# A diffusion-backbone layer on one core: TensorE in program order, side work as generators between products, opening re-ordered

## The chip, the cores and the metric

The kernel runs on one core of one Trainium2 chip. The metric is device time in microseconds (us) of one execution, as the median of several runs. A profile is one further execution, recorded by the hardware; its time stands beside the median below. Engines are named as in the profile: PE is TensorE (PEld its weight loads), DVE is VectorE, ACT is ScalarE, POOL is GpSimd, SP is the engine that issues most DMAs.

## What is computed

One layer over 256 latent tokens and 256 context tokens of width 2048, in float32. Only the latent output is returned.

```python
mod_x = split((silu(c) @ w_mod + b_mod), 6)          # shift, scale, gate, twice
h  = modulate(x,   g_mix, mod_x[0], mod_x[1])        # RMSNorm * (1 + scale) + shift
hc = modulate(ctx, g_mix, mod_c[0], mod_c[1])
qa, ka, va, qb, kb, vb, rb, lrf, lrb, gate_a, gate_b = split(h @ w_in)   # the same for hc
qa, ka = rope(rms_norm(qa)), rope(rms_norm(ka))      # 16 query heads, 4 key heads, 128 wide
o_attn = windowed_attention(qa, ka, va, ctx_k, ctx_v, sink)              # |i-j| <= 128, plus all context keys
o_gla  = latent_gla(qb, kb, vb, gf, gb, states of the context)           # 4 heads, two directions
y = sigmoid(gate_a) * (o_attn @ w_attn_o) + sigmoid(gate_b) * ((rms_norm(o_gla) * silu(rb)) @ w_gla_o)
x = x + mod_x[2] * (y @ w_out)
x = x + mod_x[5] * conv_ffn(modulate(x, g_ffn, mod_x[3], mod_x[4]))      # 2 x 5632 wide, width-3 conv, SwiGLU
```

## The kernel before

**Products.** Every big projection is a float32 product made of three: `wsplit` loads a pair of weight blocks (2 x 128 rows by 512 columns, tile `raw`, seven buffers in the pool `wr`), and `split` (L61, L62) makes a rounded part `whi` on ACT and the rest `wlo` on DVE (three buffers each). The activations are split in the same way. `proj_nat` (L167) holds the tokens stationary and streams 512 weight columns; per pair of blocks it has 12 products for two 128-token rows, 24 for four (latent and context). `proj_T` (L186) holds the weights stationary and streams 256 or 2 x 256 tokens. Results collect in four accumulator banks (`acc`); side work has three banks of its own (`side`) and one (`main`).

**Stages.** The opening computes the first shift and scale on TensorE (`mod_both`: products `pm` over `mraw` tiles of `w_mod`, a DVE transpose, then a product `pcol`), transposes x and ctx (`ptx`), makes the norm factors (`token_rows`, product `pr`), and runs the projections QB, KB, VB over groups of block rows, `(0,2) (2,2) (4,4) (8,4) (12,4)`, adding each group's result to an SBUF tile (L394). The GLA stage runs four blocks (second half of KB, three of VB) with one GLA head beside each: `gla_A` builds decayed q and k over eight levels and multiplies them (`pa`, L534 for the levels and L599 for the context part), `gla_o` makes the outputs (`po`). Then KA and VA follow, with `norm_rope` on each bank of KA and a transpose `ptk` (L711). In the attention stage the blocks QA 1 to 3 and GA run with `attend` of one group of four heads beside each. RB and the merge follow: `rb_evac`, the four rounds of GA, `w_attn_o`, GB, `w_gla_o`, each result transposed by `to_T` (`pto`, L816), then `w_out`, the turn to the FFN (a `flush()` of all that is put off, norm, split) and the FFN.

**One instance of `attend`** (one group g, one block t of 128 queries): four times three score products `pS` (L751 to L753) and a masked copy with the row maximum on DVE (L755); small DVE steps (L759 to L761); on ACT the exponential of the sink (L762) and four exponentials with their sums (L764); sum and reciprocal (L766, L767) and four scalings by it (L769) on DVE; then, for four key blocks, four transposes `ptp` (L776), a split into `pth` and `ptl`, and three products `poa` (L782 to L784).

**What sets the order.** The program is written with `tick()` at the head of every pair of weight blocks. A tick counts down what `defer(n, ...)` has put off, takes steps of one generator `beside` (1.5 steps for each tick with GLA, 1.4 with attention), and issues steps of the background `bg_steps`. `mod_latent` is that background: the later shifts and gates as multiply-adds on DVE over `raw` tiles of `w_mod` (L266), out of the same pool as the weights. A generator that is not done at the end of its block is run out there. The order in which an engine then executes is chosen by a scheduler, for all engines, TensorE too; `high_priority` marks the weight splits. `chain` keeps the loads of the opening in program order on SP.

Of the kernel before, what the change touches and what calls it, by code (L numbers as in the profile page):

```python
# [8 lines left out]
F32 = mybir.dt.float32  # L9
# [21 lines left out]
def layer_kernel(ctx, tc, A, out):  # L31
# [6 lines left out]
    wr = pool(name="wr", bufs=7)  # L38
# [39 lines left out]
    x00 = M("x00", [P, D])  # L78
    nc.sync.dma_start(x00, A["x"][0][0:P, :])
# [22 lines left out]
    def columns(name, parts, eng=G):  # L102
        rows = sm.tile([P, P], F32, name="rows", tag="t128", bufs=2)
# [5 lines left out]
        pt = bank("pt_" + name, (P, P))  # L109
        PE.transpose(pt[:, :n], rows[:n, :], ident[:n, :n])  # L110
        t = cst.tile([P, n], F32, name=name)
        V.tensor_copy(t, pt[:, :n])
        return t

    c1 = columns("c1", [A["b_mod"][0], A["g_mix"][0], A["g_ffn"][0]], nc.scalar)
    bmod, gmix, gffn = c1[:, 0:96], c1[:, 96:112], c1[:, 112:128]

# [3 lines left out]

# [10 lines left out]

    def tick():

        for e in later:
            e[0] -= 1
        while later and later[0][0] < 0:
            later.pop(0)[1]()
        if beside:
            beside[2] += beside[1]  # L140
            while beside[2] >= 1.0:
                beside[2] -= 1.0
                next(beside[0], None)
        bg_rate[1] += bg_rate[0]
        while bg_rate[1] >= 1.0 and bg_steps:
            bg_rate[1] -= 1.0
            bg_steps.pop(0)()
# [17 lines left out]
    def proj_nat(w, r0, c0, kts, lhs, evac):  # L165

        banks = [acc.tile([P, 512], F32, name="acc", tag="acc") for _ in lhs]  # L167
        for k0 in kts[::2]:
# [3 lines left out]
            for i, l in enumerate(lhs):  # L172
                for k in range(nk):
                    kt = k0 + k
                    ahi, alo = l(kt)
                    PE.matmul(banks[i], ahi, hi[:, k, :], start=(kt == kts[0]), stop=False)  # L176
                    PE.matmul(banks[i], alo, hi[:, k, :], start=False, stop=False)  # L177
            for i, l in enumerate(lhs):
                for k in range(nk):
                    kt = k0 + k  # L180
                    PE.matmul(banks[i], l(kt)[0], lo[:, k, :], start=False, stop=(kt == kts[-1]))  # L181
# [3 lines left out]
    def proj_T(w, c0, kts, rhs, evac):  # L185
# [4 lines left out]
        for k0 in kts[::2]:  # L190
            tick()
            nk = min(2, kts[-1] + 1 - k0)
            hi, lo = wsplit(w[k0 * P:(k0 + nk) * P, c0:c0 + 512])
            for part in range(2):
                for f in range(4):
                    for k in range(nk):
                        kt = k0 + k
                        w_ = (lo if part else hi)[:, k, f * P:(f + 1) * P]
                        for i, r in enumerate(rhs):
# [3 lines left out]
                            PE.matmul(o, w_, ahi, start=(kt == kts[0] and b == 0 and part == 0),  # L203
                                      stop=(kt == kts[-1] and part == 1), skip_group_check=True)
                            if part == 0:
                                PE.matmul(o, w_, alo, start=False, stop=False, skip_group_check=True)  # L206
        for i in range(len(banks)):
            evac(i, banks[i])
# [4 lines left out]
    def mod_both(part, t0, n, dst):  # L213
# [5 lines left out]
        def step(k0):  # L219
# [8 lines left out]
            if k0 == KT - nk:  # L228
                tr = W2("fb", "mtr", [P, n, 4, 32])
                V.transpose(tr.rearrange("p a b c -> p (a b c)"), a[0])  # L230
                pc = bank(f"pcol{part}_{t0}", (32, n * 4, 2))
                PE.matmul(pc, sel[:, 0:32], tr.rearrange("p a b c -> p (a b) c")[:, :, 0:2], start=True, stop=True)
                pv = pc.rearrange("p (a b) c -> p b c a", b=4)
                for b4 in range(4):
                    V.tensor_copy(dst[32 * b4:32 * b4 + 32, :, t0:t0 + n], pv[:, b4, :, :])
                b0 = part * 16 + t0
                d = dst[:, :, t0:t0 + n]
                V.tensor_tensor(d, d, bmod[:, b0:b0 + n].unsqueeze(1).to_broadcast([P, 2, n]), op=ALU.add)

        return [lambda k0=k0: step(k0) for k0 in range(0, KT, nk)]  # L240

    def mod_latent(parts):
# [11 lines left out]
        def step(i):  # L254
# [13 lines left out]
            if k0 == KT - 2:  # L268
# [15 lines left out]
                defer(3, out)  # L284
# [48 lines left out]
    groups = [(0, 2), (2, 2), (4, 4), (8, 4), (12, 4)]  # L333
    mods = [mod_both(0, t0, n, shift1) + mod_both(1, t0, n, scale1) for t0, n in groups]
# [4 lines left out]

    def load_tokens(s):  # L340
        ss = sm.tile([P, 2], F32, name="ss0", tag="ss0", bufs=2)
        for t in range(2):
            x_ = x00
            if s or t:
                x_ = M(f"x{s}{t}", [P, D])
                load(x_, A["ctx" if s else "x"][0][t * P:(t + 1) * P, :])
            if t:
                V.scalar_tensor_tensor(junk, x_, 1.0, x_, op0=ALU.mult, op1=ALU.mult, accum_out=ss[:, t:t + 1])
            else:
                S.activation(junk, x_, AF.Square, accum_out=ss[:, t:t + 1])  # L350
            for g in range(4):
                pt = bank("ptx", (P, 4, P), side=True)
                for k in range(4):
                    kt = g * 4 + k
                    PE.transpose(pt[:, k, :], x_[:, kt * P:(kt + 1) * P], ident)
                dst = xr[2 * s + g // 2][:, (g % 2) * 4:(g % 2) * 4 + 4, t * P:(t + 1) * P]
                if g % 2:
                    V.tensor_copy(dst, pt)
                else:
                    S.activation(dst, pt, AF.Copy)  # L360
        rrow1.append(token_rows("fa", f"rrow{s}", rms_scale(ss, D, [P, 2])))
# [35 lines left out]
    hh, hl = [], []  # L397
    for gi, (t0, n) in enumerate(groups):
        kts = ALL[t0:t0 + n]
        if gi == 0:  # L400
            load_tokens(0)
            for f in mods[0]:
                f()
        while bg_steps:
            bg_steps.pop(0)()
        if gi + 1 < len(groups):
            bg_steps.extend(mods[gi + 1])
            ticks = 4 * ((n + 1) // 2)
            bg_rate[:] = [1.4 * len(bg_steps) / ticks + 0.01, 0.0]
        for s in range(2):  # L410
            if gi == 0:
                if s:
                    load_tokens(1)
                hh.append([M(f"h{s}{h}hi", [P, 8, T], F32R) for h in range(2)])
                hl.append([M(f"h{s}{h}lo", [P, 8, T], F32R) for h in range(2)])
            affine_group(s, t0, n)
            if s == 0:
                if gi == 0:
                    qb0 = [W2("fc", "qb0", [P, 512]) for _ in range(4)]
                for j in range(2):  # L420
                    proj_T(w_in, QB + j * 512, kts, [h_all(0)], add_to(lambda i, j=j: qb0[2 * j + i], gi == 0))
        if gi == 0:
            kbt = M("kb0", [P, 4, 512])
            vb0 = M("vb0", [P, 4, 512])
        proj_T(w_in, KB, kts, [h_all(0), h_all(1)], add_to(lambda i: kbt[:, i, :], gi == 0))
        proj_nat(w_in, 0, VB, kts, h_xc, add_to(lambda i: vb0[:, i, :], gi == 0))

    chain.clear()


    cw0 = columns("cw0", [A["conv_w"][0, 0], A["b_gate_f"][0], A["b_gate_b"][0]])
    cw1 = columns("cw1", [A["conv_w"][0, 1]])
    cw2 = columns("cw2", [A["conv_w"][0, 2]])
# [572 lines left out]
```

## Time and profile before

| | |
|---|---|
| median of 3 runs | 2054.3 us (2053.26 to 2057.96) |
| the profiled execution, own time | 2061.47 us |
| its span | 2059.7 us |
| PE busy | 1998.4 us, 97% |
| DVE busy | 1399.2 us, 68% |
| ACT busy | 932.7 us, 45% |
| HBM read, mean rate | 409.63 MB, 200 GB/s |
| DMA in the first 1/40 of the span | 346 GB/s |

Busy times are shares of the span. The stages lie at about 0 to 214 us (opening), 214 to 527 (GLA), 527 to 575 (KA and VA), 575 to 800 (attention), 800 to 1275 (RB and merge), 1275 to 1325 (turn to the FFN), 1325 to the end (FFN). Matmuls are pipelined: the time listed for one is longer than the distance to the next, and a TensorE that is listed busy may still run at a lower granted clock.

### The profile page before, as it was taken

Reading aid. Unit: us, or ns where it says so; the run is one execution under the profiler, and the core shown is the slowest. Engines: PE = TensorE matmul, PEld = TensorE weight load, DVE = VectorE, ACT = ScalarE, POOL = GpSimd, SP = SyncE. Lnnn points to the kernel's source line nnn. Section 1 sums busy time; section 2 is a strip of 40 time slices with the busy share of each in tenths; the row PEclk is TensorE's granted clock in tenths of the full one; section 3 lists DMA queues with packets and bytes.
Section 4 is the critical chain, followed back from the end, with each engine's and each line's share of the span. In section 5 each row is a group of like instructions: output and inputs, shape, how many; then the busy total and the mean of one; then the engine's idle time right before and its main releaser. Section 6 shows DMA issues by size and latency. Waiting matters only on the chain.

```text
span 2059.7 us, 30028 instructions
## 1 busy us (share of the span) xinstructions
PE 1998.4 (97%) x11792; PEld 1727.0 (84%) x11792; DVE 1399.2 (68%) x2149; ACT 932.7 (45%) x1306; POOL 38.9 (2%) x62
## 2 busy tenths in 40 slices
PE   6999999999999999999999999899999999999998
PEld 4778888888787777788788888899999889999987
DVE  4657577887758888777776455877787455556654
ACT  4323464552345665444344444544445334445532
POOL 0001000001000000000000000000000000000000
PEclk8999999999999999999999999899999999999999
DMA  9977322346553466788886766576776666666563
GB/s 346 360 261 217 95 82 83 92 134 203 162 153 113 135 194 198 254 274 273 275 267 218 230 211 205 177 252 226 235 260 208 201 192 191 182 182 183 184 214 112
DMA packets 214350, 413.71 MB, mean 201 GB/s; under 512 B 12548, under 2 KB 21092, under 8 KB 213184
## 3 DMA queue, kind: packets, MB, share of 16 engines
q1 hardware_dynamic: 212320, 406.89, 62.0%
q0 software_dynamic: 1360, 4.74, 0.8%
q8 instruction: 92, 1.51, 0.3%
q14 instruction: 50, 0.41, 0.1%
q10 hardware_dynamic: 528, 0.17, 0.0%
HBM read 409.63 MB, written 2.11 MB: 200 GB/s over the span
## 4 chain that ended last, share of the span: by engine, by line
PE 78%; DVE 9%; DMA 8%; ACT 2%; issue 2%; DVEq 0%; POOL 0%; ACTq 0%; SPq 0%
PE acc L203 20%; PE acc L176 13%; PE acc L177 13%; PE acc L181 13%; PE acc L206 10%; DMA raw<-in_w_mod 8%; DVE wlo L62 3%; DVE macc L266 3%; PE pm L227 1%; PE pa L534 1%; PE po L620 1%; ACT whi L61 1%; PE pa L599 1%; PE ptp L776 1%; PE poa L782 0%
## 5 line engine op out<-in xcount | busy, mean ns | idle before, releaser
L61 ACT ACTIVATE whi<-raw 128x1024 fp32r<-128x1024 f32 x568 | 601.0, 1060 | 833.9 <-PE acc L177 512.4
L62 DVE TENSOR_TENSOR wlo<-raw,whi 128x1024 fp32r<-128x1024 f32 x568 | 693.9, 1226 | 359.6 <-ACT whi L61 327.0
L203 PE MATMUL acc<-h2h,whi 128*128 128x256 f32 x1408 | 347.4, 284 | 1.5 <-ACT h2h L377 1.5
L206 PE MATMUL acc<-h2l,whi 128*128 128x256 f32 x1408 | 346.9, 284 | 0.0
L266 DVE SCALAR_TENSOR_TENSOR macc<-raw,ccol,macc 128x512 f32<-128x512 f32 x240 | 180.3, 751 | 137.3 <-DMA raw<-in_w_mod 133.9
L203 PEld LDWEIGHTS acc<-h2h,whi 128*128 128x128 f32 x1408 | 271.5, 193 | 2.0 <-ACT h2h L377 1.8
L206 PEld LDWEIGHTS acc<-h2l,whi 128*128 128x128 f32 x1408 | 271.4, 193 | 0.2
L203 PE MATMUL acc<-h2h,wlo 128*128 128x256 f32 x1408 | 198.5, 284 | 1.7 <-DVE wlo L62 1.7
L203 PEld LDWEIGHTS acc<-h2h,wlo 128*128 128x128 f32 x1408 | 182.4, 193 | 1.9 <-DVE wlo L62 1.9
L176 PE MATMUL acc<-whi,h00hi 128*128 128x512 f32 x352 | 141.0, 400 | 0.9 <-DVE kb L394 0.6
L176 PE MATMUL acc<-whi,h01hi 128*128 128x512 f32 x352 | 139.8, 397 | 0.0
L177 PE MATMUL acc<-whi,h00lo 128*128 128x512 f32 x352 | 139.7, 397 | 0.0
L177 PE MATMUL acc<-whi,h01lo 128*128 128x512 f32 x352 | 137.8, 391 | 0.0
L176 PE MATMUL acc<-whi,ah 128*128 128x512 f32 x352 | 137.1, 389 | 0.0
L177 PE MATMUL acc<-whi,al 128*128 128x512 f32 x352 | 137.0, 389 | 0.0
L181 PE MATMUL acc<-wlo,h00hi 128*128 128x512 f32 x352 | 98.2, 394 | 0.0
L181 PE MATMUL acc<-wlo,h01hi 128*128 128x512 f32 x352 | 96.9, 393 | 0.5 <-DVE wlo L62 0.5
L181 PE MATMUL acc<-wlo,ah 128*128 128x512 f32 x352 | 94.1, 389 | 0.0
L176 PEld LDWEIGHTS acc<-whi,h00hi 128*128 128x128 f32 x352 | 66.7, 190 | 14.7 <-ACT h00hi L377 0.7
L181 PEld LDWEIGHTS acc<-wlo,h00hi 128*128 128x128 f32 x352 | 66.1, 189 | 13.9 <-DVE wlo L62 0.3
L181 PEld LDWEIGHTS acc<-wlo,ah 128*128 128x128 f32 x352 | 66.1, 188 | 13.8
L176 PEld LDWEIGHTS acc<-whi,ah 128*128 128x128 f32 x352 | 66.1, 188 | 13.7
(369 smaller groups left out, 3267.7 us busy)
## 6 DMA issues: line engine op xcount, KB each, us to landing
raw<-in_w_in SPq DMA_DIRECT2D x208, 512.0 KB, 4.4
raw<-in_w_up SPq DMA_DIRECT2D x176, 512.0 KB, 3.9
raw<-in_w_mod SPq DMA_DIRECT2D x128, 512.0 KB, 4.2
raw<-in_w_down SPq DMA_DIRECT2D x88, 512.0 KB, 4.3
mraw<-in_w_mod SPq DMA_DIRECT2D x32, 1024.0 KB, 12.0
raw<-in_w_attn_o SPq DMA_DIRECT2D x32, 512.0 KB, 4.7
raw<-in_w_gla_o SPq DMA_DIRECT2D x32, 512.0 KB, 5.1
raw<-in_w_out SPq DMA_DIRECT2D x32, 512.0 KB, 4.1
```

The lines of the kernel that those rows point to most:

```text
L61: S.activation(hi, src, AF.Copy)
L62: V.tensor_tensor(lo, src, hi.bitcast(F32), op=ALU.subtract)
L176: PE.matmul(banks[i], ahi, hi[:, k, :], start=(kt == kts[0]), stop=False)
L177: PE.matmul(banks[i], alo, hi[:, k, :], start=False, stop=False)
L181: PE.matmul(banks[i], l(kt)[0], lo[:, k, :], start=False, stop=(kt == kts[-1]))
L203: PE.matmul(o, w_, ahi, start=(kt == kts[0] and b == 0 and part == 0), stop=(kt == kts[-1] and part == 1), skip_group_check=True)
L206: PE.matmul(o, w_, alo, start=False, stop=False, skip_group_check=True)
L227: PE.matmul(a[0][q:q + 32, :], cS[:, kt, :], raw[:, k, :], start=(kt < 4), stop=(kt >= 12))
L266: V.scalar_tensor_tensor(a[0], raw[:, k, :], ccol[:, kt:kt + 1], a[0], op0=ALU.mult, op1=ALU.add)
L534: PE.matmul(pa[:, t, :], k2[:, dt, t * P:(t + 1) * P], q2[:, dt, tq * P:(tq + 1) * P], start=(dt == 0), stop=(dt == 1))
L599: PE.matmul(pa[:, t, :], kk[:, dt, t * P:(t + 1) * P], qq[:, dt, :], start=(i == 0 and dt == 0), stop=(i == 1 and dt == 1))
L620: PE.matmul(po, x_, y_[:, s, :], start=(n == 0), stop=(n == 11))
```

## The change

`manual_schedule` takes TensorE out of the scheduler's hands: it executes in the order of the program. The other engines are still scheduled. `tick()` now also comes between products, after every 6 of 512 columns or 12 of 256, so a pair of blocks has 2 or 4 ticks. Generators state how many ticks they pause (`yield 4.5`), several can run at once, and they run on over the ends of blocks: one for all of GLA, one for all of attention. Four-row projections take their rows in two pairs, both parts of a pair before the next. The delays of `defer` grow with the number of ticks, and due entries run whatever their place in the list. In the opening the loads and products of the first modulation come ahead of x, the second 4-row group is two groups of 2, VB stands ahead of KB, `pcol` comes a step after its `pm` products (`end`), and the small transposes of `columns` are put off. The scaling of the probabilities and the first copy of `at` go from DVE to ACT. The pool `wr` has six buffers.

```diff
-    wr = pool(name="wr", bufs=7)
+    wr = pool(name="wr", bufs=6)
...
     def tick():
...
-        while later and later[0][0] < 0:
-            later.pop(0)[1]()
-        if beside:
-            beside[2] += beside[1]
-            while beside[2] >= 1.0:
-                beside[2] -= 1.0
-                next(beside[0], None)
+        due = [e for e in later if e[0] < 0]
+        later[:] = [e for e in later if e[0] >= 0]
+        for e in due:
+            e[1]()
+        for e in list(beside):
+            e[2] += e[1]
+            while e[2] > 0:
+                n = next(e[0], None)
+                if n is None:
+                    beside.remove(e)
+                    break
+                e[2] -= n
...
+            for i2 in range(0, len(lhs), 2):
+                for part in range(2):
+                    for i in range(i2, min(i2 + 2, len(lhs))):
...
+                            if mms % 6 == 0 and mms < len(lhs) * nk * 3:
+                                tick()
...
-    groups = [(0, 2), (2, 2), (4, 4), (8, 4), (12, 4)]
+    groups = [(0, 2), (2, 2), (4, 2), (6, 2), (8, 4), (12, 4)]
+
+    def both_parts(t0, n):
+        (s0, e0), (s1, e1) = (mod_both(part, t0, n, dst) for part, dst in ((0, shift1), (1, scale1)))
+        return s0 + s1[:1] + [e0] + s1[1:] + [e1]
...
-        V.tensor_scalar(at, pa, 2.0, None, op0=ALU.mult)
+        S.activation(at, pa, AF.Copy, scale=2.0)
...
             prev = q2, k2
-            yield
+            yield 2.75
...
         V.tensor_tensor(kg, kg, kc, op=ALU.mult)
-        yield
+        yield 4
...
-    bg_rate[:] = [0.3, 0.0]
+    bg_rate[:] = [0.08, 0.0]
...
-        defer(1 + i // 2, turn)
+        defer(8 + 4 * i, turn)
...
                 sc.append(s_)
+                yield 0.34
...
             for h in range(4):
-                V.tensor_scalar(sc[h], sc[h], ds_[:, h:h + 1], None, op0=ALU.mult)
-            yield
-            yield
+                S.activation(sc[h], sc[h], AF.Copy, scale=ds_[:, h:h + 1])
+            yield 4.5
...
-        beside[:] = [attend(g, qTs), 1.4, -2.9]
-        qTs = qa_block(g + 1) if g < 3 else ga_block()
-        for _ in beside[0]:
-            pass
-        beside.clear()
-
-
-    bg_rate[0] = 0.52
+    run(attend_all())
+    for g in (1, 2, 3):
+        qa_block(g)
+    proj_nat(w_in, 0, GA, ALL, h_x, lambda t, b: S.activation(m1[0][t], b, AF.Copy))
+
+
+    bg_rate[0] = 0.24
...
-            defer(1 + t, lambda: to_T(s_, gh, gl, j, t))
+            defer(4 + 2 * t, lambda: to_T(s_, gh, gl, j, t))
...
-    bg_rate[:] = [0.36, 0.0]
+    bg_rate[:] = [0.18, 0.0]
...
+            ctx.enter_context(tc.manual_schedule(engines={mybir.EngineType.PE}))
```

Three places show what moves. The first is attention's third instance (second group, first query block) on TensorE, around its first transposes `ptp`; `acc` is the projection, `wlo` and `whi` its weights. Before:

```order
L181 MATMUL acc<-wlo,h00hi 128x512 x4
L776 MATMUL ptp<-ident,s 128x128
L176 MATMUL acc<-whi,h00hi 128x512
L177 MATMUL acc<-whi,h00lo 128x512
L776 MATMUL ptp<-ident,s 128x128
L176 MATMUL acc<-whi,h00hi 128x512
L776 MATMUL ptp<-ident,s 128x128
L177 MATMUL acc<-whi,h00lo 128x512
L776 MATMUL ptp<-ident,s 128x128
```

And of the change, at the same place:

```order
L201 MATMUL acc<-wlo,h01hi 128x512 x4
L852 MATMUL ptp<-ident,s 128x128 x4
L197 MATMUL acc<-whi,h01hi 128x512
L198 MATMUL acc<-whi,h01lo 128x512
L197 MATMUL acc<-whi,h01hi 128x512
```

The four transposes of a key block stood between products and now follow one another. From the instance's last score product to its first transpose there were 37 products of the projection and there are 24 (30 in the last five of the eight instances).

On ACT, the same instance, from the exponential of the sink `es`; `s` are the scores, `y` and `sq` the norm of another bank. Before, and then of the change:

```order
L762 ACTIVATE es<-es 128x4
L764 ACTIVATE s,ds<-s,mx 128x512 x3
L61 ACTIVATE whi<-raw 128x1024
L764 ACTIVATE s,ds<-s,mx 128x512
L685 ACTIVATE y<-acc 128x512
L687 ACTIVATE sq<-y 128x512
L61 ACTIVATE whi<-raw 128x1024
```

```order
L837 ACTIVATE es<-es 128x4
L61 ACTIVATE whi<-raw 128x1024
L839 ACTIVATE s,ds<-s,mx 128x512 x3
L61 ACTIVATE whi<-raw 128x1024
L839 ACTIVATE s,ds<-s,mx 128x512
L844 ACTIVATE s<-s,ds 128x512 x4
L61 ACTIVATE pth<-ptp 128x512 x2
```

The four scalings (L844) are new on ACT, behind the last exponential, and two weight splits stand among the exponentials.

The third place is the start of the program on TensorE, up to the first product of the projections (`h00hi`). Before, and then of the change:

```order
L355 MATMUL ptx<-ident,x_147 128x128 x16
L327 MATMUL pr<-dg,ones 128x128 x2
L227 MATMUL pm_0_193<-mraw,cS 32x256 x16
L232 MATMUL pcol_0_216<-mtr,sel 32x16
L227 MATMUL pm_0_223<-mraw,cS 32x256 x16
L232 MATMUL pcol_0_246<-mtr,sel 32x16
L227 MATMUL pm_2_270<-mraw,cS 32x256 x8
L203 MATMUL acc<-h00hi,whi 128x256
```

```order
L257 MATMUL pm_0_118<-mraw,cS 32x256 x16
L257 MATMUL pm_0_141<-mraw,cS 32x256 x8
L112 MATMUL pt_c_152<-ident,rows 128x128
L265 MATMUL pcol_0_155<-mtr,sel 32x16
L257 MATMUL pm_0_141<-mraw,cS 32x256 x8
L395 MATMUL ptx<-ident,x_175 128x128 x16
L395 MATMUL ptx<-ident,x_176 128x128 x16
L265 MATMUL pcol_0_229<-mtr,sel 32x16
L360 MATMUL pr<-dg,ones 128x128 x2
L229 MATMUL acc<-h00hi,whi 128x256
```

The modulation's products moved ahead of the transposes of x, each `pcol` behind further work, and `pr` next to the first product of the projections.

More of the change, by code (lines that the diff above doesn't have):

```diff
@@ L131, in flush, with run, drain @@
             later.pop(0)[1]()
+    def run(gen, pace=1.0, wait=0.0):
+        beside.append([gen, pace, -wait])
+    def drain():
+        while beside:
+            for _ in beside.pop(0)[0]:
+                pass
     def tick():
@@ L404, in layer_kernel @@
         while bg_steps:
             bg_steps.pop(0)()
+        if gi == 0:
+            new_h(0)
+            qb0 = [W2("fc", "qb0", [P, 512]) for _ in range(4)]
         if gi + 1 < len(groups):
[L407 to L421, printed above, removed]
+            more = both_parts(*groups[gi + 1])
+            bg_rate[:] = [1.4 * len(more) / (6 * n), 0.0]
+            if gi:
+                bg_steps.extend(more)
@@ L603, in gla_A @@
         res.extend((ats, atc))
+        yield 2
     def gla_o(h, a, vh, vl):
@@ L743, in attend @@
         for t in range(2):
+            while (g, t) not in ready:
+                yield 1
+            qT = qTs[g]
             mx = sm.tile([P, 4], F32, name="mx", tag="mx")
```

309 lines of the change are left out of this document (181 added, 128 removed).

## The prediction

> **What bounds the kernel now.** I read the head of the profile page first, then the busy time by stage, then TensorE's waits by line. Its section 4 follows back from the last instruction what released each step.
>
> ```profile
> span 2059.7 us, 30028 instructions
> PE 1998.4 (97%) x11792; PEld 1727.0 (84%) x11792; DVE 1399.2 (68%) x2149; ACT 932.7 (45%) x1306; POOL 38.9 (2%) x62
> ...
> PE 78%; DVE 9%; DMA 8%; ACT 2%; issue 2%; DVEq 0%; POOL 0%; ACTq 0%; SPq 0%
> ```
>
> TensorE is busy 97% of the span. A change that leaves the matmuls alone can gain only what TensorE waits, and whatever makes it wait longer is added to the time. The next table cuts the span at the stages: opening (to 214 us), GLA (214 to 527), KA and VA (527 to 575), attention (575 to 800), RB and merge (800 to 1275), the turn to the FFN, the FFN.
>
> ```profile
> 0.00:28.00 28.00, 14.54 (x122) 10.32 (x122) 11.54 (x37) 9.40 (x15) 0.88 (x5) 0.93 0.99 316
> 28.00:75.00 47.00, 40.96 (x293) 32.15 (x294) 23.39 (x53) 19.49 (x34) 2.09 (x4) 0.86 0.98 355
> 75.00:214.00 139.00, 136.41 (x962) 111.82 (x961) 92.67 (x164) 43.26 (x58) 6.87 (x11) 1.00 0.79 266
> 214.00:527.00 313.00, 304.49 (x1759) 259.18 (x1757) 235.00 (x426) 154.50 (x303) 26.36 (x37) 1.00 0.40 118
> 527.00:575.00 48.00, 42.99 (x187) 34.30 (x186) 28.50 (x65) 15.46 (x28) 0.00 (x0) 0.93 0.43 131
> 575.00:800.00 225.00, 223.16 (x1030) 175.51 (x1028) 182.11 (x368) 127.72 (x221) 0.00 (x0) 1.00 0.53 156
> 800.00:1275.00 475.00, 466.50 (x2084) 380.84 (x2083) 321.01 (x384) 205.25 (x225) 1.65 (x3) 0.99 0.74 242
> 1275.00:1325.00 50.00, 41.90 (x254) 37.93 (x253) 38.15 (x68) 23.90 (x38) 0.00 (x0) 0.86 0.56 172
> 1325.00:2060.00 735.00, 727.44 (x5117) 685.00 (x5116) 466.82 (x589) 333.77 (x388) 1.06 (x2) 1.00 0.64 203
> ```
>
> After the stretch come its length, the busy time of PE, PEld, DVE, ACT and POOL, the granted clock, the DMA share and GB/s. The length less the PE column is what can be won: 13.5 us up to 28 us (there the loads run at 0.99 of the DMA engines), 6.0, 2.6, 8.5 in GLA, 5.0 in KA and VA, only **1.8 in attention**, 8.5 in RB and merge. The turn (8.1) and the FFN (7.6) keep their code but for the ring and the ticks. So attention has nothing to give, and its DVE is the busiest of any stage (182 of 225 us). TensorE's waits by line, with total, number and longest:
>
> ```profile
> PE pr L327 <- DVE dg L326: 9.3, 3, 3.7
> ...
> PE ptk L711 <- DVE sq L700: 5.0, 1, 5.0
> PE pa L599 <- DVE kf L592: 4.9, 4, 2.1
> PE pcol L232 <- DVE mtr L230: 4.8, 7, 0.9
> PE pto L816 <- DVE sr L826: 3.9, 1, 3.9
> PE pa L534 <- DVE q L554: 3.4, 4, 1.5
> PE pto L816 <- DVE m L857: 3.2, 2, 2.3
> ...
> PE ptp L776 <- DVE s L769: 0.7, 1, 0.7
> ```
>
> **The change, part by part.** The work hardly changes: 32 score scalings and the four `at` copies go from DVE to ACT, two-row groups add 12 accumulations on DVE, two table loads are added on ACT. What changes is where TensorE's side work stands between the products of a projection, so each part is a sum of covers. One instance of attention (one group and one 128-query block, eight in all) gives the prices. It runs from the last score product `pS` to the first transposed probabilities `ptp`:
>
> ```profile
> 666.25 0.40 PE L753 MATMUL pS<-kTh,qT 128*128 128x512 f32 x1
> ...
> 668.05 0.68 DVE L755 CUSTOM_DVE_ANT_0 s<-pS,att 128x512 f32<-128x512 f32 x1
> ...
> 669.76 0.19 ACT L762 ACTIVATE es<-es 128x4 f32<-128x4 f32 x1
> ...
> 670.56 0.71 ACT L764 ACTIVATE s<-s,mx 128x512 f32<-128x512 f32 x1
> ...
> 671.97 1.04 ACT L61 ACTIVATE whi<-raw 128x1024 fp32r<-128x1024 f32 x1
> ...
> 672.40 0.39 PE L177 MATMUL acc<-whi,h00lo 128*128 128x512 f32 x1
> ...
> 672.92 0.71 ACT L764 ACTIVATE s<-s,mx 128x512 f32<-128x512 f32 x1
> ...
> 673.76 0.39 PE L177 MATMUL acc<-whi,h00lo 128*128 128x512 f32 x1
> ...
> 674.38 0.18 DVE L767 RECIPROCAL ds<-ds 128x4 f32<-128x4 f32 x1
> ...
> 674.60 1.68 DVE L769 TENSOR_SCALAR s<-s,ds 128x512 f32<-128x512 f32 x4
> ...
> 675.14 0.33 PE L776 MATMUL ptp<-ident,s 128*128 128x128 f32 x1
> ...
> 676.87 0.58 ACT L61 ACTIVATE pth<-ptp 128x512 fp32r<-128x512 f32 x1
> ...
> 677.91 0.68 DVE L62 TENSOR_TENSOR ptl<-ptp,pth 128x512 fp32r<-128x512 f32 x1
> ```
>
> The two projection products quoted start 1.36 us apart with six starts from one to the other: a pitch of 0.227 us (the 0.39 is a pipelined latency). The softmax chain takes 674.60 - 666.25 = 8.35 us to the start of the scaling and 10.0 to its end at 676.28. Before, 37 products (8.4 us) stood in front of `ptp`, and further ones between its four transposes, so each later scaling was covered too.
>
> *Attention, the deciding term.* In the new order 24 products stand there in the first three instances and 30 in the other five, and the four transposes then follow without a product between them. The cover, with the score product itself, is 25 x 0.227 = 5.7 us, or 31 x 0.227 = 7.0 us. The scaling is now four ACT passes. The nearest row is the ACT copy of a 128x512 tile, 0.58, against 1.68 / 4 = 0.42 on DVE, so the last scaled tile is ready 8.35 + 4 x 0.58 = 10.7 us after the score product. TensorE stands still for 3 x (10.7 - 5.7) + 5 x (10.7 - 7.0) = 33.5 us; less the 0.7 and a few tenths that it waits today, **+32.5 us**. Behind the waiting transposes stand the whole projection, `poa` and the next scores, since TensorE runs in program order; nothing slips past. Low end: the two weight splits of ACT inside the chain (1.04 each) are out of the way because the ring of split weights is full, 8.6 us, which gives 3 x 2.9 + 5 x 1.6 = 16.7. High end: the chain is 1.5 us longer, as where the q norm of the next block stands between the reductions on DVE, 45.5. I take the middle, because it is the chain that was measured, with its splits.
>
> *Opening.* A first projection's `pcol` now has eight `pm` products of the second one ahead of it, and the first `pr` has a `pcol` and transposes. Half of the 4.8 us on `pcol` goes. Of the 6.0 + 2.6 us idle in 28 to 214 us another 2.8 may go by loads that stand nearer to their use, but the DMA engines are at 0.98 there and the bytes are the same. The x tiles now load behind four blocks of `w_mod`, so the `pr` chain (9.3 us in three, 3.1 each) and the copy of the last transposes (0.6) stand in the open ahead of the first main product; a fifth block of 1.05 MB (2.9 us at 355 GB/s) no longer loads ahead of it: +0.8. Together -2.4 - 2.8 + 0.8 = **-4.5 us** (rounded up). The 12 new accumulations (12 x 0.68 = 8.2 us of DVE) lie beside products while DVE has the room that 23.39 of 47 us shows. Ends: -9 (all of the idle time), +4 (those 8.2 us come through, less what is gained).
>
> *GLA.* A pause ahead of the `kf` products becomes 4 ticks of 6 products, 24 x 0.227 = 5.4 us, where one step was 24 x 0.227 / 1.5 = 3.6 us: 1.8 us more for each of four, which is nearly all of the 4.9 on L599. Of the 3.4 on L534 a little goes with `at` on ACT. **-5 us**, ends -8.3 (both rows) and +4 (DVE, at 235 of 313 us, falls behind the even pace of the levels).
>
> *KA and VA.* `ptk` is put off by 8 ticks or more (8 x 6 x 0.227 = 10.9 us), so its 5.0 us goes, and with it the slow products behind it (rows below, 2.2 us). The fourth bank's norm still has to wait for one of six `fc` buffers, for which I leave 2 us. **-5 us**, ends -7 and -1.
>
> *RB and merge.* `pto` of the two blocks is now released 4 and 6 ticks into the next projection (5.4 and 8.2 us) where it was 1 and 2 ticks of 12 products (2.7 and 5.4). That is up to 2.7 us more cover for the waits of 3.9 and 3.2, so 4.3 us go, and 1.7 of slow clock behind the first. **-6 us**, ends -9 and -1. The weight ring of six instead of seven costs nothing I can see: loads land some 4 us after issue and six pairs are 6 x 2.7 = 16 us of products.
>
> **Sum:** -4.5 - 5 - 5 - 6 + 32.5 = +12 us. The profiled execution took 2061.47 us, its span 2059.7 and 1.8 around it, 7.2 above the median of the runs, 2054.3. I add the difference to both: some 2073 in a profile like this one, **2066 us** as a median.
>
> [...] What follows a stall of TensorE is seen in the stage of KA (first four rows, after `ptk`) and of RB (after `pto`):
>
> ```profile
> 537.50:540.00 2.50, 0.00 (x0) 0.00 (x0) 2.50 (x15) 0.22 (x2) 0.00 (x0) 0.87 0.39 142
> 540.00:542.50 2.50, 0.65 (x3) 0.65 (x4) 2.50 (x6) 0.60 (x1) 0.00 (x0) 0.50 0.00 0
> 542.50:545.00 2.50, 2.50 (x9) 2.02 (x8) 2.38 (x4) 1.12 (x2) 0.00 (x0) 0.50 0.00 0
> 545.00:547.50 2.50, 2.50 (x10) 2.00 (x9) 1.27 (x2) 1.48 (x2) 0.00 (x0) 0.76 0.00 0
> ...
> 860.00:862.50 2.50, 2.50 (x10) 2.02 (x9) 2.50 (x4) 0.60 (x1) 0.00 (x0) 0.54 0.81 241
> 862.50:865.00 2.50, 2.50 (x13) 2.05 (x11) 1.26 (x4) 1.06 (x1) 0.00 (x0) 0.78 0.72 220
> ```
>
> The granted clock falls to 0.50 and 0.54 and stays low for some 5 us. The loss is the share not granted: 0.65 x 0.5 + 2.5 x 0.5 + 2.5 x 0.24 = 2.2 us behind the 5.0 us wait, 2.5 x 0.46 + 2.5 x 0.22 = 1.7 behind the 3.9 us wait. [...]
>
> **The rivals.**
> - *The chain is shorter than its cover needs (faster).* Three of the four reductions are now done before the last score product, and with the split ring full ACT goes straight through the exponentials. Without the two splits the chain is 8.6 us; the fourth reduction began 1.8 us after its score product, behind other DVE work; take off 1.4 of that, and it is 7.2: stalls of 3 x 1.5 + 5 x 0.2 = 5.5 us, 4.5 more than now. Then the 20.5 us gained elsewhere decide: 2054.3 + 4.5 - 20.5 = 2038. It decides from the chain at which eight stalls cost 21 us, 2.6 each over a mean cover of 6.5: below about **9.1 us** the change is faster. For it: the spread scores. Against it: 10.0 us measured with the cheaper DVE scaling.
> - *The clock falls at every attention stall (slower).* Stalls of 3.7 and 5.0 us lie about the 3.9 that brought the clock to 0.54. Eight times 1.8 us is 14 us: 2066 + 14 = 2080. Against it: the attention stall is broken by transposes as each scaling ends, and may not read as one idle stretch. [...]
> - *DVE becomes the bound in the opening and GLA.* The 8.2 us of accumulations come through and the 9.5 us gained in the two stages stay away: 2066 + 17.7 = 2084. Against it: DVE's 50% and 75%.
>
> That the order stays what it was is excluded by the rows of the order shown with the change.
>
> **How the numbers follow.** Forecast 0.46, with its own range 2054 to 2078; shorter chain 0.29; clock 0.19; DVE 0.06. The 80% range goes from 2037, just under the shorter chain's time, to 2092, where the high end of attention (45.5 for 33.5) and the clock meet. A measurement of this kernel tells 0.2% (4.1 us) from no change. Faster by more: 0.26, from the shorter chain. Within: 0.03 from it and 0.07 from the forecast's lower edge, 0.10. Slower: 0.39 + 0.19 + 0.06 = 0.64.
>
> **What would show it.** Right: a new leading row, `ptp` waiting for the ACT scaling some 30 us in eight times or more, attention's PE idle time above 25 us, and `ptk`, `pto` and `kf` gone from the waits. Wrong: `ptp` below 20 us in all (first rival), PEclk under 0.95 in attention (second), PE idle time grown in the opening or GLA (third).

## The result, and the profile after

The changed kernel took 2138.9 us (2131.94 to 2142.25, 4 runs) against 2056.0 for the kernel before (2053.26 to 2057.96, 4 runs): a ratio of 1.040, interval 1.037 to 1.043. It is **slower by 83 us**, outside the range of the prediction. The profiled execution of it was the quickest of its four, 2131.94 us with a span of 2130.2, and that of the kernel before, 2061.47 us, was slower than its four runs, so the two profiles differ by only 70.5 us of span.

The head of the page after the change:

```profile
span 2130.2 us, 30255 instructions
PE 2025.0 (95%) x11860; PEld 1742.2 (82%) x11860; DVE 1399.0 (66%) x2139; ACT 955.6 (45%) x1340; POOL 41.2 (2%) x62
...
PEclk9999999999999898999999999999999999999999
...
PE 73%; DMA 10%; DVE 10%; ACT 5%; issue 2%; DVEq 0%; ACTq 0%; POOL 0%; POOLq 0%
```

TensorE's busy time grew by 26.6 us for nearly the same work (68 small products more) and its idle time from 61.3 to 105.2 us. ACT, 2% of the chain before, has 5%. Now the stages, cut where the same part of the program stands in both (KA ends some 3 us later, VA 8, everything from the merge on some 73); the columns are as in the prediction's table. Side work stands elsewhere between the products, so such a cut is good to a few us.

```profile
0.00:35.00 35.00, 15.31 (x107) 9.00 (x107) 12.15 (x37) 9.72 (x15) 2.99 (x9) 0.93 0.99 334
35.00:75.00 40.00, 37.31 (x304) 30.85 (x304) 21.98 (x50) 21.37 (x36) 0.00 (x0) 0.93 0.99 330
75.00:214.00 139.00, 135.61 (x971) 104.74 (x970) 102.34 (x196) 41.15 (x58) 7.32 (x12) 1.00 0.76 257
214.00:530.00 316.00, 309.21 (x1806) 265.60 (x1805) 217.89 (x389) 155.22 (x304) 27.61 (x35) 0.99 0.35 105
530.00:583.00 53.00, 43.51 (x191) 34.98 (x190) 32.22 (x67) 15.84 (x27) 0.00 (x0) 0.94 0.40 121
583.00:873.00 290.00, 246.79 (x1029) 192.41 (x1028) 175.16 (x338) 149.48 (x255) 0.60 (x1) 0.90 0.38 112
873.00:1348.00 475.00, 467.86 (x2089) 381.85 (x2088) 331.41 (x410) 203.98 (x220) 1.62 (x3) 1.00 0.79 258
1348.00:1397.00 49.00, 41.75 (x257) 37.41 (x256) 38.19 (x67) 24.55 (x40) 0.00 (x0) 0.90 0.57 172
1397.00:2130.00 733.00, 727.63 (x5121) 685.38 (x5119) 467.67 (x590) 334.32 (x389) 1.06 (x2) 1.00 0.66 205
```

The attention stage is 290 us where it was 225: **+65 of the 70.5 us**. Idle time there went from 1.8 to 43.2 us, busy time from 223.2 to 246.8, and the granted clock from 1.00 to 0.90. KA and VA cost 5 us more, opening and GLA together 3, the last two stages 3 less; RB and merge are where they were. What TensorE waits for in attention, by group of instructions (busy time and mean, then idle time and its releasers):

```profile
L852 PE MATMUL ptp<-ident,s 128*128 128x128 f32 x128 | 29.6, 343 | 27.7 <-ACT s L844 26.1
L825 PE MATMUL pS<-kTh,qT 128*128 128x512 f32 x32 | 13.7, 429 | 4.7 <-DVE ol L62 4.0 <-ACT qT L61 0.7
L800 PE MATMUL ptq<-ident,sq 128*128 128x128 f32 x32 | 5.4, 296 | 9.7 <-DVE sq L766 5.0 <-DVE qT L62 3.3 <-DVE mx L836 1.4
```

27.7 + 4.7 + 9.7 = 42.1 of the 43.2 us: the transposes `ptp` wait for ACT's scaling, the q transposes `ptq` for small steps on DVE (the q norm, a split, a row maximum), the scores `pS` once for a split on DVE. The instance that the prediction worked with, in the timeline after the change:

```profile
686.46 0.39 PE L827 MATMUL pS<-kTh,qT 128*128 128x512 f32 x1
...
688.65 0.21 ACT L837 ACTIVATE es<-es 128x4 f32<-128x4 f32 x1 [2.30 <-DVE es L835]
688.76 1.05 ACT L61 ACTIVATE whi<-raw 128x1024 fp32r<-128x1024 f32 x1
...
691.22 1.07 PE L201 MATMUL acc<-wlo,h01hi 128*128 128x512 f32 x4
...
691.83 1.04 ACT L61 ACTIVATE whi<-raw 128x1024 fp32r<-128x1024 f32 x1
692.78 0.71 ACT L839 ACTIVATE s<-s,mx 128x512 f32<-128x512 f32 x1
...
694.52 2.56 ACT L844 ACTIVATE s<-s,ds 128x512 f32<-128x512 f32 x4 [0.93 <-DVE ds L842]
695.29 0.33 PE L852 MATMUL ptp<-ident,s 128*128 128x128 f32 x1 [3.01 <-ACT s L844]
695.91 1.70 PE L852 MATMUL ptp<-ident,s 128*128 128x128 f32 x3 [0.29 <-ACT s L844]
```

From the last score product to the last scaled tile it is 694.52 + 2.56 - 686.46 = 10.6 us (10.7 was the estimate). The 24 products are through at 692.3, and TensorE then stands, first 3.0 us, then between the four transposes.

The eight instances are not alike. Read in the same way, the distance is 11.1, 9.4, 10.6, 14.3, 10.6, 8.3, 14.7 and 14.3 us, and all but the sixth wait ahead of their first transpose, 1.7 to 5.7 us. The two longest waits are those of the last two instances. In the seventh ACT puts copies for another block and a load of its function table (ACT_TABLE_LOAD) ahead of the scalings; in the eighth such a load stands ahead of the exponentials:

```profile
812.39 1.28 ACT L931 ACT_TABLE_LOAD   x1
...
836.14 1.28 ACT L837 ACT_TABLE_LOAD   x1
```

The clock around the third instance:

```profile
692.50:695.00 2.50, 0.00 (x0) 0.00 (x0) 1.48 (x3) 1.57 (x4) 0.00 (x0) 1.00 0.54 190
695.00:697.50 2.50, 1.64 (x5) 0.87 (x6) 0.00 (x0) 2.08 (x4) 0.00 (x0) 0.65 0.76 213
697.50:700.00 2.50, 2.50 (x8) 1.81 (x8) 0.69 (x1) 0.60 (x1) 0.00 (x0) 0.50 0.00 0
700.00:702.50 2.50, 2.50 (x9) 2.15 (x8) 0.69 (x1) 0.60 (x1) 0.00 (x0) 0.50 0.00 0
```

The stall of 3.0 us is followed by some 7 us at a clock of 0.65 to 0.50.

### The profile page after: what moved, and what is told of

It is laid out like the page before. It is cut to its first block, busy times and chain, and to the rows that moved or that the text cites. A ratio compares the mean times of both kernels' runs of the same rounds, so it can differ in the third digit from the quotient of the medians.

```text
span 2130.2 us, 30255 instructions
## 1 busy us (share of the span) xinstructions
PE 2025.0 (95%) x11860; PEld 1742.2 (82%) x11860; DVE 1399.0 (66%) x2139; ACT 955.6 (45%) x1340; POOL 41.2 (2%) x62
## 4 chain that ended last, share of the span: by engine, by line
PE 73%; DMA 10%; DVE 10%; ACT 5%; issue 2%; DVEq 0%; ACTq 0%; POOL 0%; POOLq 0%
PE acc L197 12%; PE acc L198 12%; PE acc L201 11%; PE acc L229 10%; PE acc L230 10%; PE acc L233 10%; DMA raw<-in_w_mod 9%; DVE macc L299 3%; DVE wlo L62 2%; PE pa L597 1%; ACT whi L61 1%; PE pm L257 1%; ACT s L844 1%; PE po L684 1%; ACT s L839 1%
## 5 line engine op out<-in xcount | busy, mean ns | idle before, releaser
L197 PEld LDWEIGHTS acc<-whi,h01hi 128*128 128x128 f32 x352 | 68.0, 193 | 15.2 <-issue 1.7
L198 PEld LDWEIGHTS acc<-whi,h00lo 128*128 128x128 f32 x352 | 68.3, 194 | 13.2
```

The costliest lines, as they stand in the source:

```text
L197: PE.matmul(banks[i], ahi, hi[:, k, :], start=first, stop=False)
```

## The experiments

Theory A: the loss is TensorE's program order in attention, where too little stands ahead of each waiting transpose and nothing may slip past it. The rivals were the rest of the change (scaling on ACT, generators, opening), the clock alone, and a cost of program order in every stage. Times in each section go with those of the kernel before on the same chip; these lie between 2055.7 and 2057.5 us, so that "less" and "more" are against the changed kernel's 2138.9 as it is.

### e1: TensorE scheduled again

```diff
-            ctx.enter_context(tc.manual_schedule(engines={mybir.EngineType.PE}))
```

> The changed kernel with TensorE given back to the scheduler; all else as changed. Theory A (in program order the attention stage has too few products ahead of each transpose, and nothing slips past a waiting one): the stalls of ptp, ptq and pS in attention, 56 us in all, nearly go, and the time falls from about 2139 to 2070 to 2090 us. Rival B (the placement of the generators, the ACT scaling and the new opening cost the time whoever orders TensorE): it stays above 2120 us.

Measured 2058.65 us against 2056.43 for before: ratio 1.0011, interval 0.9998 to 1.0025. One line takes back the whole loss, more than theory A had forecast. With TensorE scheduled, the rest of the change taken together moves the time by nothing measurable (e8 and e9 find a loss and a gain in it). Attention in e1, cut where the same products into `acc` stand as at 575 and 800 us in the kernel before:

```profile
572.00:796.00 224.00, 219.68 (x1017) 173.95 (x1015) 171.59 (x335) 141.66 (x240) 0.59 (x1) 1.00 0.52 155
...
L852 PE MATMUL ptp<-ident,s 128*128 128x128 f32 x128 | 22.4, 277 | 0.0
```

The first line is the stage, 224 us where before has 225; the second is the group of all 128 transposes, the last of which come behind 796 us. There is no idle time ahead of `ptp` and the clock is 1.00, with the scaling still on ACT. The chain did not become shorter: from the last score product to the last scaled tile it is 12.2 to 18.9 us in e1's eight instances, but 44 to 70 products of the projections stand ahead of the first transpose, where the changed kernel has 24 or 30.

### e2: program order in the kernel before

```diff
+            ctx.enter_context(tc.manual_schedule(engines={mybir.EngineType.PE}))
             layer_kernel(ctx, tc, aps, out)
```

> The kernel before with one line added: TensorE in program order. Theory A: much slower, since before's program writes poa right behind the split that feeds it (32 times some 1.3 us) and leaves about 3.9 us of products ahead of ptp against a chain of 8 to 10 us (8 times 4 to 6 us): 2056 + 75 to 100 = 2130 to 2160 us or more. Rival (the order of TensorE matters little, the scheduler's order is close to the program's): within 10 us of 2056.

Measured 2267.5 us in one run: 211 us more, well over the 75 to 100 expected. The waits by line:

```profile
PE pa L599 <- DVE kf L592: 23.5, 4, 6.4
PE poa L782 <- ACT pth L61: 22.4, 32, 0.7
PE ptq L731 <- DVE sq L700: 18.7, 4, 4.8
PE ptp L776 <- DVE s L769: 16.0, 12, 2.4
```

Steps whose consumer is written close behind them wait, in GLA too. So the ticks and pauses of the change, with the rest of it, do most of the work that the scheduler did: with them program order costs 80 us, without them 211.

### e3 and e4: the scaling back on DVE, and filler products

```diff
-                S.activation(sc[h], sc[h], AF.Copy, scale=ds_[:, h:h + 1])
+                V.tensor_scalar(sc[h], sc[h], ds_[:, h:h + 1], None, op0=ALU.mult)
```

> The changed kernel with the four scalings of each attention instance back on DVE. Theory A (the scaling is a part of an uncovered chain): ACT's pitch of 0.64 us becomes DVE's 0.42, 8 x 4 x 0.22 = 7 us, and some slow clock goes with it: 2128 to 2134 us. Rival (the move to ACT is what makes attention slow, because it stands behind the weight splits there): 2110 us or less. If DVE's own rows delay it, no change.

Measured 2128.6 us (before 2056.43): 10 us less than the change. The move to ACT is an eighth of the loss, as a part of the chain, not its cause.

```diff
             yield 4.5
+            fill = bank("fill")
+            for i in range(16):
+                PE.matmul(fill, kTh[:, g, 0:P], kTh[:, g, :], start=True, stop=True)
             po = bank("poa", side=True)
```

> The changed kernel with 16 filler products of 512 columns (3.6 us, results unused) ahead of the first transposes of each attention instance, so that TensorE is busy for most of the time in which it waited. Clock theory (the stalls lower the granted clock, and that costs about 10 us of the 22 us of small excess in attention): 2139 + 3 for the two instances that waited under 3.6 us, - 10 = about 2132 us, and the clock of the attention stage rises to 0.98 or more. Stall-only theory: the fillers only fill, 2139 to 2145 us.

Measured 2143.4 us (before 2056.43). The same stretch from the first q transpose to the end of attention, first of the changed kernel, then of e4:

```profile
624.00:857.00 233.00, 193.19 (x788) 148.56 (x786) 138.68 (x283) 122.67 (x221) 0.60 (x1) 0.88 0.33 96
```

```profile
630.00:863.00 233.00, 208.83 (x911) 164.50 (x912) 138.68 (x283) 121.17 (x219) 0.59 (x1) 0.94 0.32 94
```

8 x 16 x 0.227 = 29 us of useless products cost 4.5 us. Only a part of them stood where TensorE stood still: the stretch has 39.8 - 24.2 = 15.6 us less idle time. For the rest the other instructions are listed some 13 us shorter, at a clock of 0.94 instead of 0.88. The clock did not reach 0.98, and 24.2 us of idle time are left, at `ptq`, `pS` and some `ptp`. The time came out as the stall-only theory has it, but the theory's reason, that the fillers only fill, holds for half of them. The run shows a clock 0.06 higher with 15.6 us less of stalls; how much of the 13 us is the clock, and how much the longer listed time of products that stand alone (0.39 us, where dense ones start 0.227 apart), it does not tell.

### e5 and e6: program order in attention only, and everywhere else

```diff
+    order = ExitStack()
+    in_order = lambda: order.enter_context(tc.manual_schedule(engines={mybir.EngineType.PE}))
...
+    in_order()
     bg_rate[0] = 0.0
     qa_block(0)
...
         assert j == 0 or not beside
+        if j == 0:
+            order.close()
...
-            ctx.enter_context(tc.manual_schedule(engines={mybir.EngineType.PE}))
             layer_kernel(ctx, tc, aps, out)
```

(e5; e6 has `in_order()` at the head and swaps the two calls.)

> The changed kernel with TensorE in program order only in the blocks QA, GA and the first of RB, beside which attention runs; scheduled everywhere else. Theory A (the loss is attention's: its stage has 78 us of TensorE excess in program order and 16 when scheduled): 2058 + 62 = 2120 us, 2110 to 2126. Rival (program order costs a little in every stage): half or less of the 80 us, below 2098.

> The complement: TensorE in program order everywhere but in those blocks. Theory A: 2139 - 62 = 2077 us, 2070 to 2084, the rest being the wait for the key norm's buffers around KA and VA (10 us more than when scheduled). Rival (costs in every stage): above 2095.

Measured 2125.4 and 2094.9 us (before 2057.5). e5 is 67 us above e1, so attention alone brings five sixths of the loss. e6 is 36 above e1: it misses the 2077 expected and nearly meets its rival's bound, and 67 + 36 is more than 80, so the two do not add up. The traces say where the surplus lies. Every run has 10272 products into `acc`, so two runs can be compared at the same one. At the end of VA the changed kernel is 10 us behind the kernel before and e1 is 3 ahead, so program order had cost 13 us by then, 10 of them during VA. From the merge to the end neither moves by more than 4 us against the kernel before. So program order costs some 13 us outside attention, which fits 80 less 67. e6 is 11.5 us behind at the end of VA, 8.7 where the kernel before stands at 750 us, and 35.0 where it stands at 800: 26 us are lost in between, where attention runs into the first RB block, with stalls of 5.5 and 5.6 us at `ptp` in the last two instances, next to the seam between the two ways of ordering. That the seam makes them is likely, since e1 has no such stall there; moving it was not tried.

### e7 and e10: the next scores ahead of the transposes

```diff
-    wr = pool(name="wr", bufs=6)
+    wr = pool(name="wr", bufs=4)
...
-    F2_BUFS = {"fa": 4, "fb": 4, "fc": 6, "mod": 2}
+    F2_BUFS = {"fa": 8, "fb": 4, "fc": 6, "mod": 2}
...
+        for i in range(9):
+            if i < 8:
...
+                yield from attend(g, t, out)
+                todo.append((g, t, out[0]))
+            if i:
+                yield 3.0
+                yield from probs(*todo.pop(0))
```

`attend` is cut in two: scores and softmax, and `probs` (transposes and `poa`).

> The changed kernel, TensorE in program order, with the score products of the next attention instance issued ahead of the transposes of this one (eight score tiles; the weight ring is four deep to make room), and a pause of 3 ticks between. Cover theory (TensorE stalls because too little stands ahead of the transposes): 8 + 18 products and 12 score products, some 8 us against a chain of 9 to 10, so of 40 us at ptp 25 to 35 go: 2100 to 2115 us. Rival (ACT and DVE are what bounds the stage, and the stalls only move to pS, ptq or the accumulators): above 2125.

Measured 2130.4 us (before 2057.5), only 8.5 less: the rival's number. The waits by line:

```profile
PE poa L860 <- ACT pth L61: 22.2, 7, 5.9
...
PE ptq L800 <- DVE sq L766: 7.6, 3, 3.4
```

`ptp` is gone from the list and `poa` has come in its place: ACT worked at the next instance's exponentials before it copied `pth`. At the longest of these waits the transposes were through at 805.5 us, ACT did other evacuations and four exponentials, and the copy started at 810.8. So e10 marks that split as urgent:

```diff
+                    with tc.high_priority():
+                        split(th, tl, pt.rearrange("p a b -> p (a b)"))
```

> The kernel of e7 with the split of the transposed probabilities marked as urgent, so that ACT copies pth ahead of the next instance's exponentials. Theory (in e7 the stall moved from ptp to poa, 22 us, because pth stood behind those exponentials on ACT): poa waits below 10 us, and 2130 - 12 to - 20 = 2110 to 2118 us. Rival (ACT has no time to spare, and the stalls move on to the next ptp): 2125 us or more.

Measured 2100.7 us in two runs (before 2057.04), another 30 less and below the range expected. Its waits:

```profile
PE ptq L800 <- DVE sq L766: 14.3, 4, 4.5
PE pc L95 <- DMA ident<-in_k_ident: 10.8, 1, 10.8
```

Neither `ptp` nor `poa` leads any more. Program order thus keeps half of its loss with this cover, and ACT's order of work decides whether the cover is of use. The urgent split without the earlier scores was not run, so the gain is that of the two together. e7 and e10 also have the shallower ring, whose cost was not measured by itself.

### e11: other delays for two transposes

```diff
-        defer(8 + 4 * i, turn)
+        defer(3 + 3 * i, turn)
...
-            defer(5 + 2 * t, turn)
+            defer((9 if g else 5) + 2 * t, turn)
```

> The changed kernel, TensorE in program order, with the delays of two transposes changed: ptq of the blocks QA 1 to 3 four ticks later, ptk after 3, 6, 9 and 12 ticks instead of 8, 12, 16 and 20. Theory (each transpose is a wait set by a number of ticks: ptq stands too early, by 1.6 to 3.4 us in three blocks, 6.8 us; ptk too late, so that the fourth key norm waits for buffers, 7.7 us): 2139 - 10 = 2126 to 2132 us. Rival (the waits only move to what uses the transposes): 2136 us or more.

Measured 2132.5 us (before 2057.04): 6.4 less by the medians, but the ranges overlap, and the profiled executions of the two kernels have spans of 2130.5 and 2130.2 us. So the traces do not show where a gain lies. The two halves went different ways:

```profile
PE ptp L852 <- ACT s L844: 31.9, 19, 7.7
...
PE acc L197 <- ACT y L751: 7.9, 2, 7.5
...
PE ptq L800 <- DVE sq L766: 3.4, 1, 3.4
```

`ptq` fell from 9.7 us to 3.4, of which `ptp` took back 5.8 (31.9 for 26.1). The wait for the key norm's copy `y` stayed, 7.5 us where it was 7.7, so the reason given for it, late `ptk`, was wrong. The timeline of the changed kernel shows what it waits for, and behind it one row of e1:

```profile
537.16 0.75 DVE L299 SCALAR_TENSOR_TENSOR macc<-raw,ccol,macc 128x512 f32<-128x512 f32 x1 [1.97 <-DMA raw<-in_w_mod]
...
543.89 0.69 DVE L766 TENSOR_TENSOR sq<-sq,y 128x512 f32<-128x512 f32 x1
...
544.67 0.60 ACT L751 ACTIVATE y<-acc 128x512 f32<-128x512 f32 x1 [4.19 <-DVE sq L766]
```

```profile
539.66 0.60 ACT L751 ACTIVATE y<-acc 128x512 f32<-128x512 f32 x1 [4.19 <-DVE sq L766]
```

The buffer comes free with the first bank's rope on DVE, and DVE had stood in front of a background multiply-add, waiting for a `w_mod` load (here 2.0 us, at 531 us another 4.5). Taking the background out of KA was not tried. In e1 the copy waits the same 4.19 us and TensorE, which has other products to go on with, only 1.3: the late buffer is there in both, and program order turns it into a stall.

### e8, e9 and e12: the start

```diff
+    x_t = load_tokens(0)
     first = both_parts(*groups[0])
-    for f in first[:3]:
+    turn_tokens(0, 0, x_t[0])
+    turn_c1()
+    turn_tokens(0, 1, x_t[1])
+    token_factor(0)
+    for f in first:
         f()
-    turn_c1()
-    first[3]()
-    first[4]()
-    x_t = load_tokens(0)
-    turn_tokens(0, 0, x_t[0])
-    turn_tokens(0, 1, x_t[1])
-    first[5]()
-    token_factor(0)
```

All three leave TensorE to the scheduler; this is e8's edit on e1:

> The changed kernel with TensorE scheduled (2058 us) and with x loaded, transposed and normed ahead of the first modulation, as before the change. Opening theory (with the modulation first, the norm of x stands in the open ahead of the first main product, at 34 us where it was 28): 5 to 6 us less, 2051 to 2054, and so slightly faster than the kernel before. Rival (the opening is bound by its loads, and a later start is caught up by 130 us): 2056 to 2060.

Measured 2057.1 us (before 2057.5; ratio 0.9991, interval 0.9979 to 1.0004): no gain. The order of x and the modulation was not what delayed the start, as the first row of TensorE in e8 shows; behind it two rows of e9, which loads the identity and c first:

```profile
11.27 0.28 PE L95 MATMUL pc<-ident,crow 32*128 32x32 f32 x1 [11.27 <-DMA ident<-in_k_ident]
```

```profile
6.17 0.31 PE L95 MATMUL pc<-ident,crow 32*128 32x32 f32 x1 [6.17 <-ACT crow L88]
...
28.87 0.50 PE L229 MATMUL acc<-h00hi,whi 128*128 128x256 f32 x2 [3.28 <-ACT h00hi L419]
```

```diff
-    nc.scalar.dma_start(crow[0:16, :], A["c"][0].rearrange("(k p) -> k p", p=P))
-    nc.scalar.dma_start(crow[16:32, :], A["c_ctx"].rearrange("(k p) -> k p", p=P))
...
-    nc.scalar.dma_start(ident, A["k_ident"])
+    load(ident, A["k_ident"])
+    load(crow[0:16, :], A["c"][0].rearrange("(k p) -> k p", p=P))
+    load(crow[16:32, :], A["c_ctx"].rearrange("(k p) -> k p", p=P))
```

> The kernel of e8 with the identity and the rows of c loaded on SP ahead of x. Theory (in e8 the first product waits until 11.3 us for the identity, which queues behind two x tiles issued at once, where it came at 7.5 us before the change; all of the start hangs on it): the first product comes near 5 us, the first main product near 27 us instead of 33, and the time is 2057 - 4 to - 6 = 2051 to 2053 us. Rival (the opening is bound by its loads, and the earlier start is caught up by 130 us): 2055 to 2058 us.

Measured **2050.5 us** against 2057.04 (ratio 0.9966, interval 0.9954 to 0.9977): 0.3% faster than the kernel before, and 6.6 us below e8. The identity, 64 KB, took 9.5 us from issue to landing in e8, where it was issued on ACT's queue at 1.7 us and two x tiles of 1 MB on SP's ahead of it, and 2.0 us in e9, where it is issued first. The first main product moves from 33.20 us in e8 to 28.87. The last of these three puts the same loads first in the kernel before.

> The kernel before with only the loads of e9: the identity and the rows of c first on SP, then x. If e9's gain is the start alone, it comes here too: the first product at some 6 us instead of 7.5, the first main product at 27 instead of 28.3, 2057 - 1 to - 2 = 2055 to 2056 us, no measurable change. If e9 is faster by its groups and generators as well, this stays at 2055 or more while e9 has 2050; if the early identity is worth 6 us by itself, it is 2051.

Measured 2056.45 us against 2055.69 for before (ratio 1.0005, interval 0.9994 to 1.0015). There the identity had taken 5.6 us and now takes 2.0, but the first main product stays at 28.88 us (28.34 before), where it waits 2.3 us for the split of its weights. So e9's gain over e8 is the earlier start, and its gain over the kernel before lies behind the start: its GLA stage begins at 217 us and before's at 221, and its wait in VA is 0.9 us where before has 5.0. e8 has the same order behind a start that is 4.3 us later, so in e1 and e8 the late identity hides what the rest of the change wins when TensorE is scheduled. Which of the re-orderings wins it was not separated. The profiled execution of e9 was its slowest, so its trace tells where time is won and not how much.

## Why the prediction was wrong

The direction was right and the size was not: +12 us were forecast, +83 measured, 70.5 between the two profiles. The terms in turn:

- **Chain and cover of `ptp`: the mechanism right, the sum in part by luck.** In the instance chosen it was 10.7 us against a measured 10.6. But that instance had the shortest chain of the eight before (10.0; the others 10.7 to 14.4), and in the changed kernel the eight have a mean of 11.7. Of stall 33.5 us were forecast. The idle time listed is 27.7, and the transposes that stand inside the stalls are listed 7.2 us longer than in e1 (29.6 for 22.4), 34.9 together. The longer chains did not add more in part because TensorE had already waited at `ptq` behind the scores of the fourth and the sixth instance, which served as cover. e1 shows that the order makes the stall; e7, where `ptp` stops waiting, that cover takes it away.
- **"+32.5 us" as the whole of attention: the step that failed.** The stage cost 65: idle time grew by 41.4 us and busy time by 23.6. The sum asked what `ptp` waits for and let all other side work be covered as it was. In program order `ptq` and `pS` wait too, 9.7 + 4.7 = 14.4 us, nearly all of it for small steps on DVE. They had 0.3 us on the list before, and the prediction said that nothing slips past a waiting instruction without asking it of the others.
- **The clock was made a rival at 0.19 where it belonged in the sum.** It fell to 0.90 over the stage, below the 0.95 that the prediction gave as this rival's sign, and 23.6 us of busy time were added there. By the prediction's way of counting, the share not granted is 0.10 of 246.8 us, some 25, where the rival allowed 14: an estimate, since a product is listed 0.39 us where dense ones start 0.227 apart, so that products that now stand alone may make a part of the 23.6, and the clock's own share is not settled. Behind the third instance's first wait of 3.0 us the clock was 0.50 for 6.8 us (695.8 to 702.6), 6.3 of them busy: 6.3 x 0.5 = 3.2 us by the same counting, where the rival allowed 1.8 for each instance. How long TensorE must wait before the clock falls, no run tells.
- **The 20.5 us of gains in the other stages did not come.** Opening and GLA lost 3 where 9.5 were to be won, KA and VA lost 5 instead of winning 5, RB and merge won nothing instead of 6. In the opening idle time grew by 3.7 us: the identity came at 10.4 us (7.5 was the first product before), and `pr` waited 5.7 us in one piece ahead of the first main product where 3.1 was allowed. In GLA `kf` fell from 4.9 to 2.1 us of waiting, but others rose, and idle time fell by 1.7 us where 5 were to be won. In VA the wait of 5.0 us at `ptk` became 7.7 at `y`: it was put at 2.
- **First rival (chain below 9.1 us): refuted** by the mean of 11.7 us, though one instance has 8.3. **DVE as the bound: refuted.** The extra accumulations came (DVE was busy 102.3 us between 75 and 214 us, 92.7 before), but TensorE's idle time there grew by 0.8 us only. The idle time of the opening did grow, which the prediction gave as this rival's sign; 2.9 of its 3.7 us came ahead of 75 us, as much as the identity came later.
- The forecast took for granted that a fixed order with more cover in its numbers is no worse than a scheduler's in the stages that were not looked at closely. e1 shows that order alone to be worth 80 us, with the same work, generators and delays, and e5 that 67 of these are attention's.

## What to carry to other kernels

When an engine is taken from a scheduler and put in program order, list every instruction on it that waits for another engine, and hold the cover written ahead of each against the measured length of its chain; here one that was short by 3.0 us cost those, and 6.8 us at a clock of 0.50 followed. One instance does not stand for all: the chain that was measured was the shortest of eight, and with other work of ACT and DVE in it some were 4 us longer. Cover is lost on the producer's side too: ACT's order of work decided whether more products helped (2130.4 us in e7, 2100.7 in e10). A small load that all depends on goes ahead of large ones where it sets the start (6.6 us from e8 to e9), and brought nothing where the weights set it (e12, ratio 1.0005).

## What the runs showed of the hardware

In the changed kernel's third instance the clock fell after a wait of 3.0 us in front of `ptp`, from 1.00 to 0.50, and stayed there for 6.8 us, the last 5 of them dense products. Four transposes stood between the wait and these products, the first listed 0.33 us at a clock of 1.00, the others 0.47 to 0.48 at 0.50, with gaps of 0.29 and then 0.14 us; they did not keep the clock up.
